# Products of queries with the rests of the keys over all 128 array rows instead of 64, in a hybrid decoder step

## The chip, the cores and the metric

The kernel runs on one core of a Trainium2 chip. The metric is the time on the device, in microseconds (us), of one execution of the whole step. The engines of the core are TensorE (PE in the profile, its weight loads PEld), VectorE (DVE), ScalarE (ACT), GpSimd (POOL) and SyncE (SP, whose queue issues most DMAs). Each engine works through its own list of instructions in order and waits for the others by semaphores.

## The reference, cut to what matters

One layer of a decoder with two branches, on a prompt of 512 tokens plus 16 learned ones, and on 8 sample sequences of 8 tokens. Two places of the prompt's attention branch concern the change. The first scores all keys for each query, to select the best 128; the second is the attention over the selected keys:

```
def indexer_scores(qi, wi, ki):
    s = jax.nn.relu(jnp.einsum('bqhd,bsd->bqhs', qi, ki) * IDX_DIM ** -0.5)
    return jnp.einsum('bqhs,bqh->bqs', s, wi * IDX_HEADS ** -0.5)
...
    s = jnp.einsum('bqhgd,bqkhd->bqhgk', qh, k_sel) * HEAD_DIM ** -0.5
    s = jnp.where(valid[:, :, None, None, :], s, -jnp.inf)
    p = jax.nn.softmax(s, axis=-1)
    o = jnp.einsum('bqhgk,bqkhd->bqhgd', p, v_sel)
```

A head has 64 elements in both (IDX_DIM and HEAD_DIM are 64). The indexer has 8 heads and one set of keys; the attention has 16 heads of queries on 4 heads of keys.

## The kernel before

**Exact products.** TensorE multiplies in float32r, which keeps fewer bits than float32. So each operand is split into a rounded part and a rest (the difference), and a product is a sum of several matmuls into one accumulator: rounded by rounded, rest by rounded, rounded by rest. For the large projections these are three matmuls of 128 rows by 288 or 296 columns (`mm3`, line 145; its like in the state space projection is line 1029).

**The two products of the change.** A head fills only 64 of the 128 rows of the array. The kernel uses this: the query tile (`qS` in the indexer, `QS` in the attention) holds the rounded query in its head's own half of the partitions and the rest of the query in the other half. One matmul with the rounded keys in both halves (`kS`, line 356; `KS`, line 963) then gives rounded by rounded and rest by rounded together, over 128 rows. A second matmul adds rounded by rest: it takes the own half of the query tile, 64 rows, against the rest of the keys (`kL`, line 357; `KL`, line 964). In the indexer `kL` has the rest in both halves of the partitions, since `kiT` was doubled. In the attention `KL` is a tile of 128 x 2 x 528, in which each half of the partitions holds one of two heads.

**The indexer** (lines 344 to 363) goes over four tiles of 128 queries, and over 144, 272, 400 and 528 keys in them, for 8 heads; 528 keys are done as pieces of 512 and 16. ACT takes the sum out of the accumulator (line 358), DVE weighs and adds it to the scores `am` (lines 360, 362), and DVE then marks the 128 highest of each row by repeated maximum and replacement (lines 420, 421). Products of the input projection (line 145) stand between on TensorE.

**The attention** (`query`, lines 926 to 1001) goes over the four tiles of queries, two pairs of key heads (`hp`), and two pairs of queries (`gp`), each with two `g` and two `e`: 64 times one row of keys, the 528 keys as pieces of 400 and 128. DVE adds the mask and takes the maximum (line 965), ACT takes the exponential (968), DVE scales (979), TensorE transposes (985, 988) and multiplies with the values (995, 996). A `Pipe` keeps units in flight. The state space projection (line 1029) fills TensorE between them; DVE adds its results up (line 1034).

**Order.** The program is built with a scheduler that lays out each engine's list from modelled times, so an added instruction can move others. Tiles come from pools: `cp` lives through the whole kernel, `pf` and `up` end when the attention begins (`u_stack.close()`).

Of the kernel before, what the change touches and what calls it, by code (L numbers as in the profile page):

```python
# [9 lines left out]
FT = mybir.dt.float32  # L10
FR = mybir.dt.float32r
# [3 lines left out]
OP = mybir.AluOpType  # L15
# [55 lines left out]
def body(ctx, tc, a, o):  # L71
    nc = tc.nc
    SB, PS, DR = bass.MemoryType.SB, bass.MemoryType.PSUM, bass.MemoryType.DRAM
    act, dve, pool, pe, sy = nc.scalar, nc.vector, nc.gpsimd, nc.tensor, nc.sync

    WB = (2, 3)
    cp = ctx.enter_context(tc.tile_pool(name="cp", bufs=1))
# [41 lines left out]

# [1 line left out]
    def split(raw, hi, lo, lo_eng=None):  # L121
# [26 lines left out]

# [1 line left out]
    def rows(src, n):  # L150
# [8 lines left out]
    pf = u_stack.enter_context(tc.tile_pool(name="pf", bufs=1, side="right"))  # L159
# [8 lines left out]
    scT = pf.tile([128, 24, 24], FT, name="scT")  # L168
    cwT = cp.tile([128, 120], FT, name="cwT")
    nwT = cp.tile([128, 16], FT, name="nwT")  # L170
    xp, xs, meta = a["x_prompt"][0], a["x_sample"].rearrange("b s d -> (b s) d"), a["meta_tokens"]
# [26 lines left out]
    for t in range(5):  # L198
# [7 lines left out]
        for q in range(2):  # L206
# [7 lines left out]
            dve.tensor_tensor(ul[:, 4 * q:4 * q + 4, 128 * t:128 * t + n], pv[:, :, :n], h_.bitcast(FT), op=OP.subtract)  # L214
    # convolution: weights and earlier rows, channels on partitions
    cwr = p0.tile([128, 128], FT, name="cwr")
# [21 lines left out]

# [1 line left out]
    d_g = drp.tile([2, 8, 128, NQ], FT, name="d_g")  # L240
# [34 lines left out]

    # page rows
    idx = cp.tile([128, 8], I32, name="idx")
    idx2 = cp.tile([128, 8, 2], I32, name="idx2")
    dts = cp.tile([128, 5, 32], FT, name="dts")
    acum = cp.tile([128, 5, 32], FT, name="acum")  # L280
    wdt = cp.tile([128, 5, 32], FT, name="wdt")
    elast = cp.tile([128, 4, 32], FT, name="elast")
    elc = cp.tile([128, 16, 8], FT, name="elc")
    dsc = cp.tile([128, 16], FT, name="dsc")
    for e in range(2):
        src = a["d_skip"]
        sy.dma_start(dsc[64 * e:64 * e + 64], bass.AP(tensor=src.tensor, offset=src.offset + e, ap=[[0, 64], [2, 16]]))
    wds = cp.tile([96, 2, 32], FT, name="wds")

    with tc.tile_pool(name="p1", bufs=1) as p1:  # L290
# [23 lines left out]

        # index queries of the prompt: the rounded part in a head's own half of the partitions, the rest in the other
        qS = p1.tile([128, 8, NP], FR, name="qS")
# [13 lines left out]

        # page rows of the sample sequences
        pt = p1.tile([128, 64], I32, name="pt")
# [10 lines left out]

# [1 line left out]
        wis = p1.tile([128, 4, 8], FT, name="wis")  # L345
        dve.tensor_scalar(wis, sm_tok[:, 0:4, 64:72], 8 ** -0.5, None, op0=OP.mult)
        for t in range(4):
            L = LT[t]
            sc = am[:, LO[t]:LO[t] + L]
            for h in range(8):  # L350
                ct, e = divmod(h, 2)
                lq, own = qS[:, h, 128 * t:128 * t + 128], slice(64 * e, 64 * e + 64)
                r = p1.tile([128, 528], FT, tag="ri", name="ri", bufs=2)
                for c0, c1 in pieces(L):
                    ps = mis()
                    pe.matmul(ps[:, :c1 - c0], lq, kS[:, c0:c1], start=True, stop=False)
                    pe.matmul(ps[:, :c1 - c0], lq[own], kL[own, c0:c1], start=False, stop=True)
                    act.activation(r[:, c0:c1], ps[:, :c1 - c0], AF.Relu, scale=0.125)
                if h == 0:
                    dve.tensor_scalar(sc, r[:, :L], wis[:, t, 0:1], None, op0=OP.mult)  # L360
                else:
                    dve.scalar_tensor_tensor(sc, r[:, :L], wis[:, t, h:h + 1], sc, op0=OP.mult, op1=OP.add)
            dve.tensor_tensor(sc[:, L - 128:L], sc[:, L - 128:L], K("neg"), op=OP.add)

# [1 line left out]
        QIz = p1.tile([128, 4, 128], FT, name="QIz")  # L366
# [47 lines left out]

# [1 line left out]
        m8 = p1.tile([128, 4, 8], FT, name="m8")  # L416
# [7 lines left out]

        # time steps and decays
        brow = p1.tile([128, 2, 32], FT, name="brow")
# [59 lines left out]

# [1 line left out]
        kvT = [KT[:, 0, :], KT[:, 1, :]]  # L488
# [15 lines left out]

# [1 line left out]
        for kp in range(8):  # L506
# [95 lines left out]

# [1 line left out]
    with tc.tile_pool(name="p3", bufs=1, reuse_waits="tile") as p3, \  # L604
# [11 lines left out]
        def start(g):  # L616
# [10 lines left out]
            pool.tensor_tensor(h8(G.xt4[64:80]), h8(G.xt4[64:80]), bc8(wdt[64:80, 4, g8], 16), op=OP.mult)  # L627
            # sample tokens: three rows of products a token, half the sequences at a time
            xb = p3s.tile([96, 2, 512], FT, tag="sT", name="xb", bufs=1)
# [177 lines left out]

# [1 line left out]
    for gt in (0, 1):  # L809
# [95 lines left out]
    with tc.tile_pool(name="p2h", bufs=1, reuse_waits="tile", side="right") as p2h, \  # L905
            tc.tile_pool(name="p2r", bufs=1, reuse_waits="tile") as p2r, \
            tc.tile_pool(name="p2q", bufs=1, reuse_waits="tile") as p2q, \
            tc.tile_pool(name="p2", bufs=1, reuse_waits="tile") as p2:
        # keys: rounded in both halves of the partitions, and the rest
        KS = p2h.tile([128, 4, 528], FR, name="KS")  # L910
        KL = p2h.tile([128, 2, 528], FR, name="KL")
        for kv in range(4):
            hp, e = divmod(kv, 2)
            h = slice(64 * e, 64 * e + 64)
            for i in range(2):
                act.copy(KS[64 * i:64 * i + 64, kv, :], KT[h, hp, 0:528])
            pool.tensor_tensor(KL[h, hp, :], KT[h, hp, 0:528], KS[h, kv, :].bitcast(FT), op=OP.subtract)

        # values of the last 16 keys of a tile: for both e in a half of the rows each, in parts for one product
        VZr = p2h.tile([32, 256], FT, name="VZr")  # L920
# [5 lines left out]
        def query(t, hp, gp):  # L926
            # queries 128t.., heads 8hp + 4e + 2gp + g
            L, nk = LT[t], t + 1
# [26 lines left out]
            for g in range(2):  # L955
                P2 = p2q.tile([128, 2, 528], FT, tag="P", name="P2", bufs=3)
                mx = p2q.tile([128, 2, 6], FT, tag="mx", name="mx", bufs=4)
                for e in range(2):
                    lq = QS[:, 2 * gp + g, e, :]
                    h = slice(64 * e, 64 * e + 64)  # L960
                    for i, (c0, c1) in enumerate(cuts):
                        v = pst("s")[:, :c1 - c0]
                        pe.matmul(v, lq, KS[:, 2 * hp + e, c0:c1], start=True, stop=False)
                        pe.matmul(v, lq[h], KL[h, hp, c0:c1], start=False, stop=True)  # L964
                        dve.tensor_tensor_reduce(P2[:, e, c0:c1], v, at[:, c0:c1], 1.0, NEG, OP.add, OP.max,
                                                 accum_out=mx[:, e, i:i + 1])
                    dve.tensor_scalar(mx[:, e, 2:3], mx[:, e, 0:1], mx[:, e, len(cuts) - 1:len(cuts)], -0.125, op0=OP.max, op1=OP.mult)
                    act.activation(P2[:, e, :L], P2[:, e, :L], AF.Exp, scale=0.125, bias=mx[:, e, 2:3],
                                   accum_out=mx[:, e, 3:4])
# [33 lines left out]
        Pipe().run(query(t, hp, gp) for t in range(4) for hp in range(2) for gp in range(2))  # L1003
# [1 line left out]
    HALVES = ((0, HQ), (HQ, NQ))  # L1005
# [38 lines left out]
    def rest(hi, lo, c0, c1):  # L1044
        # where the rest of tokens c0.. goes: that of the sample tokens beside their rounded part
        return [(lo[:, c0:min(c1, NP)], c0, min(c1, NP))] + ([(hi[:, NQ:NQ + NS], NP, NQ)] if c1 == NQ else [])
# [20 lines left out]
    y_stack.close()  # L1067
    # rows of the stream: four tiles of tokens, and the sample tokens: their sums with the rounded part, and with the rest
    p4 = ctx.enter_context(tc.tile_pool(name="p4", bufs=1, reuse_waits="tile", side="right"))
# [9 lines left out]
    def row_weights(src, r0, n, at=(p4w, ("dl", "dh"), 7)):  # L1079
        # n blocks of 128 rows of weights  # L1080
        return [[flat(x) for x in weights([(flat, src[r0 + 128 * k:r0 + 128 * k + 128, :])], at)] for k in range(n)]
# [12 lines left out]
    def row_norm(t, i):  # L1094
        # tokens of tile t and what scales them; i: column of the sums
        n = 128 if t < 4 else 64
# [42 lines left out]
    def last(t):  # L1139
        # the same by the pieces in which the last product ends  # L1140
        y, sq = h2[:, ORDER[0], :], h2[:, ORDER[1], :]
# [12 lines left out]
    def add_product(t, xh, xl, ws, cuts=((0, 512), (512, 1024))):  # L1154
        # rows of tile t += the product over blocks of channels
        tok = slice(128 * t, 128 * t + 128)
# [24 lines left out]
    p4a_stack.close()  # L1181
# [1 line left out]
    p5 = ctx.enter_context(tc.tile_pool(name="p5", bufs=1, reuse_waits="tile"))  # L1183
# [70 lines left out]
```

## Time and profile before

| | |
|---|---|
| times of the kernel before, us | 1586.87, 1586.79, 1581.91; median 1586.79 |
| the profiled execution | span 1586.9 us, the time of that run 1586.87 us |
| PE busy | 1488.5 us (94%), 9957 matmuls |
| DVE, ACT, POOL busy | 1006.5 (63%), 668.6 (42%), 721.2 us (45%) |
| the chain that ended last | PE 66%; DVE 14%; DMA 7%; ACT 4% |

Matmuls are pipelined, and the profile gives a matmul a duration from its start to its modelled end, so the durations of neighbours overlap. What a matmul costs the engine is read from the distance between its start and the start of the next one.

### The profile page before, as it was taken

What the parts mean: (1) busy time and instruction counts of PE and PEld (TensorE: products, weight loads), DVE (VectorE), ACT (ScalarE), POOL (GpSimd) and SP (SyncE); (2) the same over time, 40 slices, a digit from 0 to 9 for tenths busy, and PEclk for the clock granted to TensorE, in tenths of its full rate; (3) what the DMA queues carried; (4) which work ended last, traced back from release to release, by engine and by line L of the source; (5) the groups of instructions that cost most, each with busy time, mean ns of one, the idle gap of its engine ahead of it and who ended that gap; (6) DMA issues with size and microseconds to landing.
All of it is one profiled execution on the core that took longest, in us unless ns stands there. A gap on an engine that the chain in (4) does not pass through costs nothing.

```text
span 1586.9 us, 26540 instructions
## 1 busy us (share of the span) xinstructions
PE 1488.5 (94%) x9957; PEld 1308.9 (82%) x9957; DVE 1006.5 (63%) x1902; ACT 668.6 (42%) x1484; POOL 721.2 (45%) x641
## 2 busy tenths in 40 slices
PE   3899999899999899899999999998998999999998
PEld 2878999888878888779778877787797988998896
DVE  3579999967867776470444778765366445554544
ACT  3444354456655455343555555432144222332221
POOL 1523244556775675565534754335226334433322
PEclk8899999999999999999999999999999999999999
DMA  4413464687886886868873522135314222322311
GB/s 130 124 41 80 137 176 134 176 255 191 244 230 166 233 231 172 241 169 247 267 256 129 149 76 67 42 86 180 87 55 132 80 73 87 107 74 60 93 40 67
DMA packets 300160, 221.55 MB, mean 140 GB/s; under 512 B 46376, under 2 KB 269912, under 8 KB 300008
## 3 DMA queue, kind: packets, MB, share of 16 engines
q1 hardware_dynamic: 294784, 200.98, 44.8%
q0 software_dynamic: 5248, 18.88, 3.4%
q8 instruction: 78, 1.28, 0.3%
q14 instruction: 50, 0.41, 0.1%
HBM read 174.98 MB, written 44.07 MB: 138 GB/s over the span
## 4 chain that ended last, share of the span: by engine, by line
PE 66%; DVE 14%; DMA 7%; ACT 4%; issue 3%; POOL 1%; SPq 1%; POOLq 0%; DVEq 0%; ACTq 0%
PE w L145 19%; PE s L1166 13%; PE a L145 10%; PE w L1029 7%; DVE ca L574 3%; DMA bc<-d_ac 2%; PE s L964 2%; DVE scs L522 2%; PE s L861 2%; DVE m8s L521 1%; DVE r L1190 1%; PE s L726 1%; PE s L995 1%; PE a L985 1%; ACT wh L122 1%
## 5 line engine op out<-in xcount | busy, mean ns | idle before, releaser
L123 POOL TENSOR_TENSOR wl<-wr,wh 128x1024 fp32r<-128x1024 f32 x129 | 310.5, 2408 | 365.9 <-ACT wh L122 343.5
L145 PE MATMUL w<-uh,wh 128*128 128x288 f32 (+1 forms) x1168 | 361.9, 310 | 20.1 <-ACT rb L558 6.9
L145 PE MATMUL w<-ul,wh 128*128 128x288 f32 (+1 forms) x1168 | 359.2, 308 | 0.1
L145 PE MATMUL w<-uh,wl 128*128 128x288 f32 (+1 forms) x1168 | 355.6, 304 | 0.0
L145 PEld LDWEIGHTS w<-uh,wh 128*128 128x128 f32 x1168 | 225.3, 193 | 29.4 <-ACT rb L558 8.1
L145 PEld LDWEIGHTS w<-ul,wh 128*128 128x128 f32 x1168 | 225.7, 193 | 5.6 <-issue 4.4
L145 PEld LDWEIGHTS w<-uh,wl 128*128 128x128 f32 x1168 | 225.1, 193 | 3.8 <-issue 2.8
L122 ACT ACTIVATE wh<-wr 128x1024 fp32r<-128x1024 f32 x129 | 136.2, 1056 | 146.9 <-PE w L145 56.7
L123 POOL TENSOR_TENSOR dl<-wr,dh 128x1024 fp32r<-128x1024 f32 x40 | 99.3, 2485 | 154.6 <-ACT dh L122 149.8
L145 PE MATMUL a<-u2h,wh 128*128 128x288 f32 (+2 forms) x512 | 151.4, 296 | 0.7 <-ACT r L1189 0.7
L145 PE MATMUL a<-u2l,wh 128*128 128x288 f32 (+2 forms) x512 | 151.2, 296 | 0.0
L145 PE MATMUL a<-u2h,wl 128*128 128x288 f32 (+2 forms) x512 | 150.3, 294 | 0.0
L1168 DVE TENSOR_TENSOR h<-h,s 128x512 f32<-128x512 f32 (+1 forms) x101 | 67.1, 678 | 124.5 <-PE s L1166 123.8
L1166 PE MATMUL s<-dh,hh 128*128 128x512 f32 (+1 forms) x324 | 127.1, 393 | 5.9 <-DVE h L1168 5.9
L1166 PE MATMUL s<-dl,hh 128*128 128x512 f32 (+1 forms) x324 | 126.2, 390 | 0.0
L574 DVE SCALAR_TENSOR_TENSOR ca<-rb,cwT,ca 128x616 f32<-128x616 f32 x72 | 95.7, 1329 | 21.0 <-ACT ca L572 20.4
L122 ACT ACTIVATE dh<-wr 128x1024 fp32r<-128x1024 f32 x40 | 42.2, 1056 | 150.4 <-PE s L1166 128.7
L1190 DVE TENSOR_TENSOR r<-r 128x288 f32<-128x288 f32 (+2 forms) x64 | 70.1, 1096 | 52.6 <-ACT r L1189 52.6
L1166 PE MATMUL s<-dh,hl 128*128 128x512 f32 (+1 forms) x260 | 101.8, 392 | 0.0
L145 PEld LDWEIGHTS a<-u2h,wh 128*128 128x128 f32 x512 | 96.0, 188 | 1.5 <-ACT r L1189 0.9
L145 PEld LDWEIGHTS a<-u2l,wh 128*128 128x128 f32 x512 | 96.1, 188 | 0.6
L145 PEld LDWEIGHTS a<-u2h,wl 128*128 128x128 f32 x512 | 96.2, 188 | 0.0
(370 smaller groups left out, 3340.7 us busy)
## 6 DMA issues: line engine op xcount, KB each, us to landing
wr<-in_w_in_dram SPq DMA_DIRECT2D x64, 512.0 KB
wr<-in_w_up_dram SPq DMA_DIRECT2D x32, 512.0 KB
wr<-in_w_down_dram SPq DMA_DIRECT2D x32, 512.0 KB
st<-in_state_ssm_dram SPq DMA_DIRECT2D x16, 512.0 KB
bc<-d_ac SPq DMA_DIRECT2D x32, 256.0 KB
out_dram<-st SPq DMA_DIRECT2D x16, 512.0 KB
wr<-in_w_ssm_proj_dram SPq DMA_DIRECT2D x16, 512.0 KB
d_xd<-th SPq DMA_DIRECT2D x16, 296.0 KB
```

What stands on the lines that cost most here:

```text
L122: act.activation(hi, raw, AF.Copy)
L123: (lo_eng or pool).tensor_tensor(lo, raw, hi.bitcast(FT), op=OP.subtract)
L145: pe.matmul(ps[:, :c1 - c0], p[:, k, :], x[:, c0:c1], start=(k == 0 and i == 0), stop=(k == 7 and i == 2))
L521: dve.max(m8, scs)
L522: dve.match_replace(scs, m8, scs, MARK)
L574: dve.scalar_tensor_tensor(ca[:, 0:616], rb[:, k:k + 616], cwT[:, 24 * k + ct:24 * k + ct + 1], ca[:, 0:616], op0=OP.mult, op1=OP.add)
L861: pe.matmul(v[64 * hp:64 * hp + 64], QZ[:, hp, :], kk, start=True, stop=True)
L964: pe.matmul(v, lq[h], KL[h, hp, c0:c1], start=False, stop=True)
L1029: pe.matmul(ps[:, :HQ], p[:, k, mc], x[k][:, c0:c1], start=(k == 0 and i == 0), stop=(k == 3 and i == 2))
L1166: pe.matmul(ps, x, w[:, cc], start=(k == 0 and i == 0), stop=(k == len(ws) - 1 and i == len(terms) - 1))
L1168: dve.tensor_tensor(h2[:, t, cc], h2[:, t, cc], ps, op=OP.add)
L1190: dve.tensor_tensor(r, r, r, op=OP.mult)
```

## The change

In both places the second matmul takes the whole query tile and keys of 128 rows. In the indexer this needs no new data: the other half of `kL` holds the rest of the keys too, so the product of rest by rest comes in as a fourth part. In the attention `KL` gets a plane of its own for each of the four key heads, whose other half is filled with zeros by four memsets on POOL. Apart from this, nine small tiles (952 columns of float32 in all) move from the pool `cp` to the pool `pf`, and comments go, which shifts line numbers by one from line 351 to 915 and again from line 960.

```
-    cwT = cp.tile([128, 120], FT, name="cwT")
+    cwT = pf.tile([128, 120], FT, name="cwT")
...
-                ct, e = divmod(h, 2)
-                lq, own = qS[:, h, 128 * t:128 * t + 128], slice(64 * e, 64 * e + 64)
+                lq = qS[:, h, 128 * t:128 * t + 128]
...
                     pe.matmul(ps[:, :c1 - c0], lq, kS[:, c0:c1], start=True, stop=False)
-                    pe.matmul(ps[:, :c1 - c0], lq[own], kL[own, c0:c1], start=False, stop=True)
+                    pe.matmul(ps[:, :c1 - c0], lq, kL[:, c0:c1], start=False, stop=True)
...
         KS = p2h.tile([128, 4, 528], FR, name="KS")
-        KL = p2h.tile([128, 2, 528], FR, name="KL")
+        KL = p2h.tile([128, 4, 528], FR, name="KL")
...
-            pool.tensor_tensor(KL[h, hp, :], KT[h, hp, 0:528], KS[h, kv, :].bitcast(FT), op=OP.subtract)
+            pool.memset(KL[64 - 64 * e:128 - 64 * e, kv, :].bitcast(FT), 0.0)
+            pool.tensor_tensor(KL[h, kv, :], KT[h, hp, 0:528], KS[h, kv, :].bitcast(FT), op=OP.subtract)
...
                         pe.matmul(v, lq, KS[:, 2 * hp + e, c0:c1], start=True, stop=False)
-                        pe.matmul(v, lq[h], KL[h, hp, c0:c1], start=False, stop=True)
+                        pe.matmul(v, lq, KL[:, 2 * hp + e, c0:c1], start=False, stop=True)
```

Up to the attention no engine's list changes but for the shapes of these operands. In the attention the lists of all engines are laid out anew. On POOL, where the keys of the attention are prepared (`KL` the rests of the keys, `wl` the rest of a block of weights, `QS` the query tile), before:

```order
L123 TENSOR_TENSOR ysl<-yw,ysh 128x576
L123 TENSOR_TENSOR wl<-wr,wh 128x1024
L917 TENSOR_TENSOR KL<-KT,KS 64x528 x4
L123 TENSOR_TENSOR wl<-wr,wh 128x1024
L949 TENSOR_TENSOR QS<-R_9488,QS 64x4x128 x2
```

and now, in the same place:

```order
L123 TENSOR_TENSOR ysl<-yw,ysh 128x576
L123 TENSOR_TENSOR wl<-wr,wh 128x1024
L916 MEMSET KL 64x528 x4
L917 TENSOR_TENSOR KL<-KT,KS 64x528 x4
L123 TENSOR_TENSOR wl<-wr,wh 128x1024
L949 TENSOR_TENSOR QS<-R_9492,QS 64x4x128 x2
```

All four memsets stand in one block ahead of the four subtractions. On PE the first product of the attention, among those of the state space projection (`w` its accumulators, `ysh` and `ysl` its values, `wh` and `wl` its weights), before:

```order
L1029 MATMUL w_11410<-ysh_11234,wl_11363 128x288
L963 MATMUL s_9501<-KS_9466,QS_9489 128x144
L964 MATMUL s_9501<-KL_9467,QS_9489 128x144
L1029 MATMUL w_11430<-ysh_11216,wh_11426 128x288
L1029 MATMUL w_11430<-ysl_11217,wh_11426 128x288
```

and now:

```order
L1028 MATMUL w_11434<-ysh_11232,wl_11429 128x288
L1028 MATMUL w_11434<-ysh_11238,wh_11430 128x288
L1028 MATMUL w_11434<-ysl_11239,wh_11430 128x288
L1028 MATMUL w_11434<-ysh_11238,wl_11429 128x288
L962 MATMUL s_9505<-KS_9466,QS_9493 128x144
L963 MATMUL s_9505<-KL_9467,QS_9493 128x144
```

The accumulator `w_11434` is the `w_11430` of before (numbers are higher by four). Its block of twelve matmuls, of which the last four are shown, has moved from behind the first pair of query products to ahead of it.

## Rows read from the trace of the kernel before

**Rows 1.** The page's chain of work that ended last, by engine.

```profile
PE 66%; DVE 14%; DMA 7%; ACT 4%; issue 3%; POOL 1%; SPq 1%; POOLq 0%; DVEq 0%; ACTq 0%
```

**Rows 2.** Busy time by stretch of the execution: stretch and its length in us, then busy us (and instructions) of PE, PEld, DVE, ACT and POOL, the granted clock of TensorE, the DMA share, GB/s. The first two hold the indexer, the fifth the attention.

```profile
57.00:87.00 30.00, 26.79 (x167) 24.30 (x165) 19.33 (x40) 13.20 (x34) 14.92 (x12) 0.94 0.44 128
87.00:133.00 46.00, 46.00 (x244) 35.20 (x244) 40.23 (x116) 21.83 (x57) 11.49 (x7) 1.00 0.21 46
133.00:212.00 79.00, 78.37 (x573) 72.53 (x572) 78.62 (x175) 33.91 (x74) 22.90 (x16) 1.00 0.53 140
212.00:304.00 92.00, 87.32 (x636) 85.79 (x635) 89.36 (x102) 45.76 (x104) 45.33 (x47) 0.98 0.49 140
880.00:1036.00 156.00, 156.00 (x945) 120.20 (x945) 119.07 (x419) 81.10 (x226) 76.69 (x152) 1.00 0.27 78
970.00:980.00 10.00, 10.00 (x60) 7.02 (x59) 9.62 (x30) 5.88 (x16) 5.70 (x10) 1.00 0.23 65
304.00:312.00 8.00, 3.80 (x29) 3.56 (x27) 8.00 (x12) 1.95 (x3) 2.50 (x2) 0.96 0.51 144
312.00:320.00 8.00, 8.00 (x50) 7.07 (x51) 5.01 (x9) 4.97 (x11) 4.92 (x7) 0.62 1.00 326
```

**Rows 3.** The matmuls of lines 964 and 357 by source line: count, shortest, median and longest duration in ns, first and last start, and how often each form.

```profile
L964 PE MATMUL s<-KL,QS x80: 322/388/450, 880.5 to 1035.4; 64*128 64x400 f32 x32, 64*128 64x144 f32 x16, 64*128 64x272 f32 x16, 64*128 64x128 f32 x16
...
L357 PE MATMUL s<-kL,qS x20: 332/448/502, 61.8 to 122.3; 64*128 64x512 f32 x8, 64*128 64x144 f32 x4, 64*128 64x272 f32 x4, 64*128 64x400 f32 x4
...
L357 PE MATMUL a<-kL,qS x20: 273/330/452, 62.3 to 122.9; 64*128 64x16 f32 x8, 64*128 64x144 f32 x4, 64*128 64x272 f32 x4, 64*128 64x400 f32 x4
```

**Rows 4.** PE in order of time in the attention, a pair of 400 columns: start in us, duration, line, names, the part of the array (rows*columns), the moving operand.

```profile
960.82 0.29 PE L1029 MATMUL w<-ysh,wl 128*128 128x288 f32 x1
960.95 0.34 PE L963 MATMUL s<-KS,QS 128*128 128x400 f32 x1
961.22 0.45 PE L964 MATMUL s<-KL,QS 64*128 64x400 f32 x1
961.60 0.40 PE L1029 MATMUL w<-ysh,wh 128*128 128x288 f32 x1
961.84 0.29 PE L1029 MATMUL w<-ysl,wh 128*128 128x288 f32 x1
```

**Rows 5.** The same view in the indexer, a pair of 512 columns, and pairs of 144 and 272 in a row.

```profile
84.81 0.23 PE L356 MATMUL s<-kS,qS 128*128 128x144 f32 x1
84.96 0.33 PE L357 MATMUL s<-kL,qS 64*128 64x144 f32 x1
85.22 0.39 PE L356 MATMUL s<-kS,qS 128*128 128x272 f32 x1
85.55 0.39 PE L357 MATMUL s<-kL,qS 64*128 64x272 f32 x1
85.86 0.39 PE L356 MATMUL s<-kS,qS 128*128 128x272 f32 x1
...
110.34 0.40 PE L356 MATMUL s<-kS,qS 128*128 128x512 f32 x1
110.67 0.49 PE L357 MATMUL s<-kL,qS 64*128 64x512 f32 x1
111.09 0.40 PE L145 MATMUL w<-ul,wh 128*128 128x296 f32 x1
```

**Rows 6.** The same view near the end of the kernel, where only matmuls of 128 rows follow each other, of 512 and of 256 columns.

```profile
1574.00 0.39 PE L1166 MATMUL s<-dh,hh 128*128 128x512 f32 x1
1574.22 0.39 PE L1166 MATMUL s<-dh,hl 128*128 128x512 f32 x1
...
1576.75 0.28 PE L1166 MATMUL s<-dh,hh 128*128 128x256 f32 x1
1576.86 0.28 PE L1166 MATMUL s<-dh,hl 128*128 128x256 f32 x1
```

**Rows 7.** The same view in the attention, around a matmul of 96 rows (line 996).

```profile
927.30 0.36 PE L996 MATMUL s<-PR,VZ 96*128 96x256 f32 x1
927.50 0.30 PE L1029 MATMUL w<-ysh,wh 128*128 128x288 f32 x1
927.63 0.29 PE L1029 MATMUL w<-ysl,wh 128*128 128x288 f32 x1
```

**Rows 8.** Groups of DVE's instructions in the attention (880 to 1036 us): count, busy us, mean ns, idle time before them and what ended it.

```profile
L965 DVE CUSTOM_DVE_ANT_0 P<-s,am 128x400 f32<-128x400 f32 (+2 forms) x80 | 33.6, 432 | 13.9 <-PE s L964 11.1 <-PE a L985 1.0 <-POOL ts L977 0.7
...
L970 DVE RECIPROCAL mx<-mx 128x2 f32<-128x2 f32 x31 | 5.1, 163 | 6.8 <-ACT P L968 6.6
```

**Rows 9.** POOL in order of time where the keys are prepared, with the idle time ahead of an instruction and what ended it in brackets; and the group of the nearest memset.

```profile
868.57 1.32 POOL L917 TENSOR_TENSOR KL<-KT,KS 64x528 fp32r<-64x528 f32 x1 [0.52 <-ACT KS L916]
870.57 4.12 POOL L917 TENSOR_TENSOR KL<-KT,KS 64x528 fp32r<-64x528 f32 x3 [0.67 <-ACT KS L916]
875.60 2.40 POOL L123 TENSOR_TENSOR wl<-wr,wh 128x1024 fp32r<-128x1024 f32 x1 [0.91 <-ACT wh L122]
...
L1075 POOL MEMSET h<- 64x1024 f32 x1 | 1.0, 951 | 0.1
```

**Rows 10.** DVE in order of time, the first instruction that it waited for after the indexer (idle time ahead of it, and what ended it, in brackets).

```profile
215.69 1.70 DVE L574 SCALAR_TENSOR_TENSOR ca<-rb,cwT,ca 128x616 f32<-128x616 f32 x1 [2.20 <-ACT ca L572]
```

More of the change, by code (lines that the diff above doesn't have):

```diff
@@ L168, in body @@
     scT = pf.tile([128, 24, 24], FT, name="scT")
-    cwT = cp.tile([128, 120], FT, name="cwT")
-    nwT = cp.tile([128, 16], FT, name="nwT")
+    cwT = pf.tile([128, 120], FT, name="cwT")
+    nwT = pf.tile([128, 16], FT, name="nwT")
     xp, xs, meta = a["x_prompt"][0], a["x_sample"].rearrange("b s d -> (b s) d"), a["meta_tokens"]
@@ L278, in body @@
     idx2 = cp.tile([128, 8, 2], I32, name="idx2")
[L279 to L284, printed above, removed]
+    dts = pf.tile([128, 5, 32], FT, name="dts")
+    acum = pf.tile([128, 5, 32], FT, name="acum")
+    wdt = pf.tile([128, 5, 32], FT, name="wdt")
+    elast = pf.tile([128, 4, 32], FT, name="elast")
+    elc = pf.tile([128, 16, 8], FT, name="elc")
+    dsc = pf.tile([128, 16], FT, name="dsc")
     for e in range(2):
@@ L287, in body @@
         sy.dma_start(dsc[64 * e:64 * e + 64], bass.AP(tensor=src.tensor, offset=src.offset + e, ap=[[0, 64], [2, 16]]))
-    wds = cp.tile([96, 2, 32], FT, name="wds")
+    wds = pf.tile([96, 2, 32], FT, name="wds")
     with tc.tile_pool(name="p1", bufs=1) as p1:
@@ L959, in query @@
                     lq = QS[:, 2 * gp + g, e, :]
-                    h = slice(64 * e, 64 * e + 64)
                     for i, (c0, c1) in enumerate(cuts):
```

## The prediction

> **What bounds the kernel now.** I read the chain of waits first: two thirds of the span end in TensorE's own work [rows 1]. Then the busy times by stretch, for the two places that the change touches [rows 2]. In the attention (880 to 1036 us) PE is busy for all 156.00 us and DVE for 119.07, at full granted clock (2.4 GHz): nothing but PE's own list sets the pace. In the indexer it is mixed. From 87 to 133 us PE is full (46.00 of 46) and DVE idles for 46 - 40.23 = 5.8 us; from 133 to 212 both are full, DVE with 78.62 of 79; from 212 to 304 DVE has 89.36 of 92 and PE less. So what PE saves in the indexer runs into a DVE that is busy for the next 170 us, while what it saves in the attention goes straight to the end, as long as DVE keeps up.
>
> **What a 64-row matmul costs now.** A busy PE tells nothing here, since durations overlap; the distance between starts does. Where only 128-row matmuls follow each other, 512 columns take 0.22 to 0.23 us and 256 take 0.11 [rows 6], and 288 take 0.13 [rows 7]. The reader should now see three things around the 64-row matmul of 400 columns [rows 4]:
> - the 128-row matmul before it (L963) takes 961.22 - 960.95 = 0.27, where 400 columns are worth 0.18 (between the 0.13 of 288 and the 0.23 of 512): 0.09 too much;
> - it takes itself 961.60 - 961.22 = 0.38: 0.20 too much;
> - the next (L1029) takes 961.84 - 961.60 = 0.24 instead of 0.13: 0.11 too much.
>
> Together 0.40 us for a pair. The third is the telling one: L1029 has no operand or accumulator in common with the query products, and pays for standing behind one. Behind the 96-row matmul of line 996, which the profile gives as 96*128, the same L1029 takes 0.13 [rows 7]. So it is the step to 64 rows and back that costs: PE ends what it has before it loads the next weights. The Trainium skill has a rule that speaks against a gain (TensorE: Matmul & The Clock Gate, Why this matters for your kernels): a single matmul of few rows takes the same time as one of 128. By that rule the sum below would be 0; by rows 4 it is 0.40 a pair. No row here shows 64-row matmuls behind each other; where the two kinds alternate, the trace doesn't bear the rule out.
>
> The other sizes in the same way. For 272 columns, between two 64-row ones, L356 takes 0.33 and L357 0.31 [rows 5], both worth 0.13 at 128 rows: 0.20 + 0.18, about 0.39. For 512, 0.33 and 0.42 against 0.23 each [rows 5], and 0.11 behind it: 0.40. For 144, 0.15 and 0.26 [rows 5]; no row shows so short a product among 128-row ones, so I take the 0.11 of 256 columns as its floor: 0.04 + 0.15 + 0.11 = 0.30; for 128 the same. For the 16-wide pieces of the indexer I take half of 0.40, an estimate.
>
> **The change, part by part.**
> - *Attention, second product over 128 rows.* 32 pairs of 400, 16 of 272, 16 of 144, 16 of 128 [rows 3]: 32 x 0.40 + 16 x 0.39 + 32 x 0.30 = 28.6 us of PE's 156. That leaves 127.4, and DVE's 119.07 below it [rows 2]. DVE's waits for PE shrink with it (11.1 us for L964 alone), but its waits for ACT's exponential do not: 6.8 us before the reciprocal [rows 8]. 119.1 + 6.8 = 125.9, just under PE's 127.4, and in 970 to 980 us DVE already has 9.62 of 10 [rows 2]. Two engines so nearly even, tied in order through three accumulators, won't both run without a gap. I charge 1.2 us for that stretch (9.62 less the 8.4 that PE would want with four pairs of 400 shortened) and half of the 6.8, 3.4 us: 28.6 - 4.6 = 24. Bounds: 28.6 if DVE hides all, 14 if half is lost.
> - *Indexer, second product over 128 rows.* 8 pairs each of 512, 400, 272, 144 and 16 columns [rows 3]: 8 x (0.40 + 0.40 + 0.39 + 0.30 + 0.20) = 13.5 us of PE. What is late next is DVE. The first pairs, from 61.8 us on, fall where PE also waits for others (26.79 busy of 30 [rows 2]); from 87 us on, DVE can come forward by no more than its idle 5.8 us, and, at 215.69, by the 2.20 us in which it waited for ACT [rows 10]. So 0 to 13.5, and I take 6, near DVE's idle time.
> - *Four memsets on POOL.* The nearest row is 0.95 us for 64 x 1024 [rows 9], so 0.5 each for 64 x 528, 2 us in a block ahead of the four subtractions. POOL finished its weights at about 868.0 and waited 0.52 and 0.67 for ACT's KS; the subtractions took 5.4 [rows 9]. With the memsets first they run from 870.1 to 875.5 instead of to 874.7, and the weights behind them started at 875.60, after 0.91 of waiting for ACT [rows 9]. So nothing moves: the cover is that wait, and without it the cost is at most 2 us, once, for the weights and query tile queued behind it. The memsets wait for PE's last reads of the memory they write, as ACT's KS does; a longer wait would go the same way.
> - *Order.* The block of twelve matmuls ahead of the first query product is work that PE does anyway; at about 875 to 880 us it only gives POOL's query tile more time. Bounds of the new lists as a whole: 2 us either way, and I take 0. The tiles that changed pools are read and written as before: 0.
>
> **Sum.** The profiled execution took 1586.87 us with a span of 1586.9, so nothing lies around the span, and it stands at the median of 1586.79 (the lowest of the three runs is 1581.91). 1586.9 - 24 - 6 = 1557 us.
>
> **Rivals.**
> - *PE's saving arrives in full.* 28.6 + 13.5 = 42: 1545 us. For it: DVE's work that PE needs is a small part in the indexer, most is the marking of the best keys, which nobody needs before the attention. Against it: DVE does its list in order, and PE's needs stand between.
> - *DVE becomes the bound in both places.* Half of the attention's 28.6 and nothing of the indexer: 1573 us. For it: DVE at 0.76 of the attention's time and 0.99 of 133 to 212 us. Against it: a third of DVE's idle time in the attention is a wait for the very product that gets shorter [rows 8].
> - *The row count is not what costs.* Then the second product over 128 rows would stop the engine as the one over 64 does, because of its accumulator or its repeated query tile, and the time stays within 2 us of 1587. For it: only query products show the 0.38, and always in such pairs. Against it: the L1029 behind a pair shares neither with it and pays 0.11 [rows 4], but nothing behind 96 rows [rows 7]. The Trainium skill's rule above would give the same 1587.
> - *TensorE's clock falls in the attention: slower.* After 304 to 312 us, in which PE was busy for only 3.80 of 8, it was granted 0.62 in the mean of the next 8 us, so most of them at 1.2 GHz instead of 2.4 [rows 2]. If PE now waits for DVE in the attention and half of its 127.4 us of work comes at 0.62, it takes 63.7 + 63.7 / 0.62 = 166, 10 us more than now; with 6 from the indexer, 1591. It decides from a mean below 127.4 / (156 + 6) = 0.79. Against it: PE would still be busy for nine tenths of the stretch, and 212 to 304 us, with PE that busy, stands at 0.98 [rows 2].
>
> **How the numbers follow.** The forecast as summed has a chance of 0.62, with a range of its own of 1549 to 1565; the full saving 0.12; DVE as the bound 0.18; the row count without effect 0.05; the slower clock 0.03. The range of 1545 to 1573 takes in the first three. About 0.3% (5 us) is what a measurement of this kernel tells from no change: faster than that 0.92, within it 0.05, slower 0.03.
>
> **What would show it.** The start-to-start distances: L962 and L963 of 400 columns at 0.18 each and the following projection matmul at 0.13; the attention at about 132 us from its first query product to its last, instead of 155; the PE-paced start of the state space part at 304 us some 6 us earlier, with DVE without idle time between 87 and 212. It is wrong if a matmul behind the second product still takes 0.24 (then it was not the rows), or if those distances are right but PE shows waits for DVE's L964 or L978 that add up to more than 14 us (then DVE is the bound).

## The result, and the profile after

The changed kernel takes 1548.93 us (median of 4 runs, 1545.86 to 1551.57), the kernel before 1585.62 on the same chip (4 runs): a ratio of 0.9775, 95% interval 0.9755 to 0.9794. That is 36.7 us less; the prediction had 30 less, 1557, and a range of 1545 to 1573. The time lies inside that range, and at the edge of the narrower one that the sum had of its own (1549 to 1565). The profiled execution of the changed kernel took 1551.57 us, with a span of 1549.8.

The first view is the chain of work that ended last. Against [rows 1] the share that ends in PE has fallen from 66 to 58%, and DVE's has grown from 14 to 19%:

```profile
PE 58%; DVE 19%; DMA 8%; ACT 5%; issue 4%; SPq 2%; POOL 2%; POOLq 0%; DVEq 0%; ACTq 0%
```

Busy time by stretch, columns as in [rows 2]; the first four hold the indexer and what follows it, the last the attention:

```profile
57.00:82.00 25.00, 21.70 (x148) 21.29 (x149) 18.75 (x36) 10.82 (x28) 13.01 (x10) 0.93 0.50 148
82.00:122.00 40.00, 38.05 (x256) 35.07 (x255) 37.07 (x111) 23.31 (x60) 9.94 (x6) 1.00 0.21 43
122.00:202.00 80.00, 79.07 (x576) 73.17 (x575) 79.62 (x181) 33.50 (x73) 25.30 (x18) 1.00 0.53 145
202.00:296.00 94.00, 88.48 (x641) 86.76 (x640) 91.33 (x102) 45.94 (x105) 45.05 (x49) 0.98 0.48 136
867.00:997.00 130.00, 129.13 (x948) 114.72 (x947) 115.92 (x416) 78.36 (x226) 76.84 (x152) 1.00 0.33 94
```

The attention's two engines are now nearly even, 129 us of PE and 116 of DVE in 130, and PE still waits for nothing to speak of (0.87 us). The second products by source line, as in [rows 3], show the stretch: from 867.8 to 995.8 it is 128.0 us, where it was 154.9.

```profile
L963 PE MATMUL s<-KL,QS x80: 272/290/432, 867.8 to 995.8; 128*128 128x400 f32 x32, 128*128 128x144 f32 x16, 128*128 128x272 f32 x16, 128*128 128x128 f32 x16
...
L356 PE MATMUL s<-kL,qS x20: 229/343/396, 63.3 to 110.9; 128*128 128x512 f32 x8, 128*128 128x144 f32 x4, 128*128 128x272 f32 x4, 128*128 128x400 f32 x4
```

PE in order of time around a pair of 400 columns, which answers to [rows 4], and around a pair of 128 columns:

```profile
942.65 0.29 PE L1028 MATMUL w<-ysl,wh 128*128 128x288 f32 x1
942.78 0.34 PE L962 MATMUL s<-KS,QS 128*128 128x400 f32 x1
942.96 0.34 PE L963 MATMUL s<-KL,QS 128*128 128x400 f32 x1
943.14 0.29 PE L1028 MATMUL w<-ysh,wl 128*128 128x288 f32 x1
943.28 0.29 PE L1028 MATMUL w<-ysh,wh 128*128 128x288 f32 x1
...
962.58 0.22 PE L962 MATMUL s<-KS,QS 128*128 128x128 f32 x1
962.64 0.27 PE L963 MATMUL s<-KL,QS 128*128 128x128 f32 x1
962.75 0.35 PE L1028 MATMUL w<-ysh,wh 128*128 128x288 f32 x1
962.94 0.27 PE L987 MATMUL a<-cst,ts 128*96 128x128 f32 x1
```

From start to start the pair of 400 takes 0.18 and 0.18, and the projection matmul behind it 0.14 (942.78, 942.96, 943.14, 943.28): the 0.27, 0.38 and 0.24 of [rows 4] are gone, by 0.39 us in all. The pair of 128 takes 0.06 and 0.11, and what stands behind it 0.19: the weight loads (PEld) of this stretch start 0.11 to 0.14 us apart, more than the 0.06 that 128 columns take, so part of the cost stays. In the indexer, as in [rows 5]:

```profile
82.99 0.23 PE L355 MATMUL s<-kS,qS 128*128 128x144 f32 x1
83.06 0.28 PE L356 MATMUL s<-kL,qS 128*128 128x144 f32 x1
83.17 0.33 PE L355 MATMUL s<-kS,qS 128*128 128x272 f32 x1
83.34 0.28 PE L356 MATMUL s<-kL,qS 128*128 128x272 f32 x1
83.46 0.29 PE L355 MATMUL s<-kS,qS 128*128 128x272 f32 x1
...
101.94 0.39 PE L355 MATMUL s<-kS,qS 128*128 128x512 f32 x1
102.17 0.40 PE L356 MATMUL s<-kL,qS 128*128 128x512 f32 x1
102.41 0.30 PE L145 MATMUL w<-ul,wh 128*128 128x296 f32 x1
```

512 columns take 0.23 and 0.24, 144 take 0.07 and 0.11. DVE's groups in the attention (867 to 997 us), as in [rows 8], show that its wait for the query products has all but gone, from 13.9 to 1.9 us, and that for ACT's exponential has stayed:

```profile
L964 DVE CUSTOM_DVE_ANT_0 P<-s,am 128x400 f32<-128x400 f32 (+2 forms) x79 | 31.9, 429 | 1.9 <-PE s L963 1.5 <-POOL ts L976 0.4
...
L969 DVE RECIPROCAL mx<-mx 128x2 f32<-128x2 f32 x31 | 5.1, 163 | 7.3 <-ACT P L967 7.1
```

POOL where the keys are prepared, and the first wait of DVE after the indexer, which answer to [rows 9] and [rows 10]:

```profile
854.12 2.25 POOL L916 MEMSET KL<- 64x528 f32 x4
856.34 5.58 POOL L917 TENSOR_TENSOR KL<-KT,KS 64x528 fp32r<-64x528 f32 x4
861.99 2.41 POOL L123 TENSOR_TENSOR wl<-wr,wh 128x1024 fp32r<-128x1024 f32 x1
```

```profile
205.92 1.69 DVE L573 SCALAR_TENSOR_TENSOR ca<-rb,cwT,ca 128x616 f32<-128x616 f32 x1 [2.23 <-ACT ca L571]
```

The four memsets take 2.25 us, and the subtractions follow without a wait. DVE's wait for ACT at the start of the convolution, 2.20 us before, is 2.23 now: it came forward with everything else and gave nothing back.

### The profile page after: what moved, and what is told of

Its sections match the earlier page's. It is cut to its first block, busy times and chain, and to the rows that moved or that the text cites. A ratio compares the mean times of both kernels' runs of the same rounds, so it can differ in the third digit from the quotient of the medians.

```text
span 1549.8 us, 26550 instructions
## 1 busy us (share of the span) xinstructions
PE 1455.0 (94%) x9957; PEld 1302.2 (84%) x9957; DVE 1005.0 (65%) x1902; ACT 665.6 (43%) x1484; POOL 722.3 (47%) x645
## 4 chain that ended last, share of the span: by engine, by line
PE 58%; DVE 19%; DMA 8%; ACT 5%; issue 4%; SPq 2%; POOL 2%; POOLq 0%; DVEq 0%; ACTq 0%
PE s L1165 16%; PE w L145 12%; PE a L145 11%; PE w L1028 6%; DVE ca L573 3%; DVE scs L521 2%; PE s L860 2%; DVE m8s L520 2%; DVE am L420 1%; DMA bc<-d_ac 1%; DVE am L361 1%; DVE m L419 1%; DVE r L1189 1%; ACT wh L122 1%; PE s L725 1%
## 5 line engine op out<-in xcount | busy, mean ns | idle before, releaser
L1167 DVE TENSOR_TENSOR h<-h,s 128x512 f32<-128x512 f32 (+1 forms) x101 | 67.2, 678 | 128.0 <-PE s L1165 126.9
L122 ACT ACTIVATE dh<-wr 128x1024 fp32r<-128x1024 f32 x40 | 42.4, 1059 | 154.9 <-PE s L1165 132.1
```

What stands on the lines that cost most here:

```text
L122: act.activation(hi, raw, AF.Copy)
L1167: dve.tensor_tensor(h2[:, t, cc], h2[:, t, cc], ps, op=OP.add)
```

## The experiments

The table has what was read from each run: the time and its ratio to the runs of before of the same chip, and from the profiled execution the last indexer product into an accumulator `s` (line 357; the one into `a` comes 0.2 to 0.7 us later), the last marking of the sample scores (522), the time from there to the first copy of the attention's keys (916), from that copy to the last product with the values (996), and from there to the last product of the feed-forward (1166, hidden by rounded weights). All are starts, in us, and lines are those of before. Before itself took 1585.30 us on the chip of e1 to e4 (13 runs), 1586.72 on that of e5, e7, d1 and d2 (17) and 1584.88 on that of e8 and e9 (9).

| run | time (runs) | ratio, 95% interval | last indexer product | last marking | to key copy | attention | behind it |
|---|---|---|---|---|---|---|---|
| before | 1585.62 (4) | | 122.3 | 308.0 | 559.9 | 175.9 | 535.3 |
| after | 1548.93 (4) | 0.9775, 0.9755 to 0.9794 | 110.9 | 299.5 | 554.4 | 149.6 | 538.8 |
| e1 indexer alone | 1577.83 (10) | 0.9959, 0.9933 to 0.9986 | 111.0 | 298.4 | 558.8 | 175.9 | 532.2 |
| e2 attention alone | 1559.58 (4) | 0.9833, 0.9785 to 0.9881 | 120.7 | 306.8 | 555.6 | 149.7 | 538.6 |
| e3 rows alone | 1552.95 (4) | 0.9788, 0.9732 to 0.9844 | 110.3 | 297.4 | 559.2 | 152.3 | 536.5 |
| e4 both on 64 rows | 1569.93 (2) | 0.9899, 0.9835 to 0.9962 | 117.3 | 302.8 | 559.1 | 165.8 | 535.7 |
| e5 tiles alone | 1585.39 (12) | 1.0000, 0.9981 to 1.0018 | 122.8 | 308.9 | 556.1 | 176.2 | 537.7 |
| e7 rows and tiles | 1553.24 (6) | 0.9801, 0.9768 to 0.9834 | 110.1 | 298.0 | 559.5 | 152.1 | 540.1 |
| d1 few marks, 64 rows | 1588.73 (1) | | 120.2 | 279.8 | 587.9 | 175.9 | 536.0 |
| d2 few marks, 128 rows | 1581.29 (1) | | 109.3 | 268.1 | 590.4 | 176.0 | 537.6 |
| e8 96 rows | 1550.09 (1) | | 110.5 | 297.5 | 553.1 | 150.9 | 539.4 |
| e9 after again | 1552.14 (5) | 0.9789, 0.9768 to 0.9811 | 109.5 | 297.5 | 555.1 | 151.0 | 538.0 |

**Each place alone.** The kernel before with the indexer's second product on 128 rows:

```
-                    pe.matmul(ps[:, :c1 - c0], lq[own], kL[own, c0:c1], start=False, stop=True)
+                    pe.matmul(ps[:, :c1 - c0], lq, kL[:, c0:c1], start=False, stop=True)
```

> Kernel before with the 128-row second product in the indexer alone. My theory (stepping from 128 to 64 rows and back costs about 0.4 us a pair, and DVE's list takes part of what TensorE saves here): 8 to 11 us faster than before, about 1576; the attention unchanged, 155 us from its first query product to its last. Rival (TensorE's 13.5 us arrive in full): 13 to 14 us faster. Rival (DVE takes it all): no change.

and the changed kernel with that line, and the two that serve it, put back as before:

```
-                lq = qS[:, h, 128 * t:128 * t + 128]
+                ct, e = divmod(h, 2)
+                lq, own = qS[:, h, 128 * t:128 * t + 128], slice(64 * e, 64 * e + 64)
...
-                    pe.matmul(ps[:, :c1 - c0], lq, kL[:, c0:c1], start=False, stop=True)
+                    pe.matmul(ps[:, :c1 - c0], lq[own], kL[own, c0:c1], start=False, stop=True)
```

> The changed kernel with the indexer's second product back at 64 rows. Theory: 27 us faster than before (24 to 30), about 1558; 128 us from the first to the last query product of the attention, and the stretch before it as in the kernel before. If the two places were not independent, the gains of this run and of the indexer alone would not add up to the 36 us of the whole change.

The indexer alone gave 0.41% (1585.30 to 1577.83 us), 7.5 us, just under the 8 to 11 that I had expected; the attention alone 1.67% (to 1559.58), 25.7 us, within the 24 to 30. Together 2.08%, some 33 us: within the interval of the whole change, 2.06 to 2.45%, at its lower end, and neither needs the other. In the table each shortens its own stretch by as much as both do: the last indexer product comes at 111.0 with and without the attention's half, the attention takes 149.7 and 149.6 us with and without the indexer's.

**The rows without what goes with them.** The kernel before with the two matmuls widened, and nothing else: `KL` keeps its two planes, so that the other half of the rows holds the rests of the other head's keys, under the rests of the query. No zeros, no memsets, no tiles moved, and the order of before. It adds the product of the rests of the query with the rests of another head's keys, which the reference doesn't have.

```
-                    pe.matmul(ps[:, :c1 - c0], lq[own], kL[own, c0:c1], start=False, stop=True)
+                    pe.matmul(ps[:, :c1 - c0], lq, kL[:, c0:c1], start=False, stop=True)
...
-                        pe.matmul(v, lq[h], KL[h, hp, c0:c1], start=False, stop=True)
+                        pe.matmul(v, lq, KL[:, hp, c0:c1], start=False, stop=True)
```

> The kernel before with nothing but the two matmuls widened to 128 rows: in the attention the other half of the rests then belongs to the other key head, so a product of rest by rest of two different heads is added, which is tiny; no memsets, no larger tile, no tiles moved between pools. Theory (the rows alone make the gain): the time of the changed kernel, 1549, within 3 us. Rival (the new order of the attention, the memsets or the pools have a part in the gain): 4 us or more away from it, on either side.

1552.95 us, 0.9788: two shapes of operands carry the gain. The 4.0 us to the 1548.93 of the changed kernel are just over the 3 that I had allowed, but that one was measured beside other runs of before; the two ratios lie within each other's intervals, and so does that of the changed kernel measured again (e9, below). By source line its second products span 131.6 us, against 128.0 with the new order and 154.9 before:

```profile
L964 PE MATMUL s<-KL,QS x80: 272/289/351, 869.2 to 1000.8; 128*128 128x400 f32 x32, 128*128 128x144 f32 x16, 128*128 128x272 f32 x16, 128*128 128x128 f32 x16
```

**Both products on 64 rows.** If it is the step between 64 and 128 rows that costs, a pair that stays on 64 rows should pay it once in and once out, and where a pair stands right behind another, not between them. The version leaves out the product of the rest of the query with the rounded keys, in both places:

```
-                    pe.matmul(ps[:, :c1 - c0], lq, kS[:, c0:c1], start=True, stop=False)
+                    pe.matmul(ps[:, :c1 - c0], lq[own], kS[own, c0:c1], start=True, stop=False)
...
-                        pe.matmul(v, lq, KS[:, 2 * hp + e, c0:c1], start=True, stop=False)
+                        pe.matmul(v, lq[h], KS[h, 2 * hp + e, c0:c1], start=True, stop=False)
```

> The kernel before with both products of a pair over 64 rows; the product of the rest of the query with the rounded keys is left out. Theory (the cost is that of the step in and out, once a pair): the time of before within 6 us, and the first product of a pair followed by the second at 0.18 us for 400 columns. Rival (each 64-row matmul pays for itself): the first product takes about 0.38 too, 120 more such matmuls, 25 to 40 us slower than before.

It took 1569.93 us, 15.4 less than before on the same chip. I had expected the time of before within 6 us, and had not thought of the pairs that follow each other. PE in order of time, a lone pair and then two pairs in a row:

```profile
972.09 0.39 PE L996 MATMUL s<-PR,VZ 96*128 96x256 f32 x1
972.40 0.45 PE L963 MATMUL s<-KS,QS 64*128 64x400 f32 x1
972.69 0.34 PE L964 MATMUL s<-KL,QS 64*128 64x400 f32 x1
972.96 0.40 PE L1029 MATMUL w<-ysl,wh 128*128 128x288 f32 x1
973.20 0.30 PE L1029 MATMUL w<-ysh,wl 128*128 128x288 f32 x1
...
1000.18 0.34 PE L964 MATMUL s<-KL,QS 64*128 64x400 f32 x1
1000.36 0.21 PE L963 MATMUL s<-KS,QS 64*128 64x128 f32 x1
1000.42 0.27 PE L964 MATMUL s<-KL,QS 64*128 64x128 f32 x1
```

Going in, the first 64-row product takes 972.69 - 972.40 = 0.29 instead of 0.18, 0.11 more; going out, the last takes 0.27, 0.09 more, and the L1029 behind it 0.24 instead of 0.13, 0.11 more. The 96-row matmul ahead of the pair pays the 0.09 as well: 972.40 - 972.09 = 0.31, where 0.22 is its distance to a 128-row product in the run on 96 rows below. So each change of row count costs 0.20 us: 0.09 on the matmul that ends and 0.11 on the one that begins. The weight loads of before show what is lost there, around the pair of [rows 4]:

```profile
960.82 0.19 PEld L963 LDWEIGHTS s<-KS,QS 128*128 128x128 f32 x1
961.22 0.18 PEld L964 LDWEIGHTS s<-KL,QS 64*128 64x128 f32 x1 [0.21 <-issue]
961.60 0.19 PEld L1029 LDWEIGHTS w<-ysh,wh 128*128 128x128 f32 x1 [0.20 <-issue]
```

The weights of L963 are loaded from 960.82 on, 0.13 ahead of their matmul (960.95). Those of the 64-row product, and those of L1029 behind it, start only with their matmuls (961.22 and 961.60), after PEld has idled for 0.2. On 128 rows in the changed kernel the load of the second product starts at 942.78, 0.18 ahead of its matmul. A lone 64-row matmul pays two such changes, which is the 0.40 of [rows 4]; a 64-row product behind another of the same head takes 0.18 for 400 columns and 0.06 for 128 (1000.18, 1000.36, 1000.42), as on 128 rows. In before 24 of the attention's 80 pairs stand right ahead of another, and 12 of the 40 of the indexer; 24 x 0.40 = 9.6 and 12 x 0.40 = 4.8 us should go, and the table has 175.9 - 165.8 = 10.1 for the attention and 122.3 - 117.3 = 5.0 for the indexer.

That agreement is in part luck. The changes of row count are not all that went: where two pairs in a row belong, by the order of the kernel's loops, to the two heads `e`, which lie on opposite halves of the rows, they run side by side; the pieces of one head (400 and 128 columns, 512 and 16) run behind each other. A view of such a place (x2 stands for two matmuls in a row of the same names):

```profile
965.03 0.29 PE L1029 MATMUL w<-ysh,wh 128*128 128x288 f32 x1
965.25 0.45 PE L963 MATMUL s<-KS,QS 64*128 64x400 f32 x2
965.54 0.34 PE L964 MATMUL s<-KL,QS 64*128 64x400 f32 x2
965.82 0.40 PE L1029 MATMUL w<-ysl,wh 128*128 128x288 f32 x1
```

The two first products start within 0.01 us of each other, and so do the two second ones; two pairs take 965.82 - 965.25 = 0.57, and the lone pair above took 972.96 - 972.40 = 0.56. There are 16 such places in the attention of e4 and 6 in its indexer. At what a pair of its columns takes on 128 rows in e3 (0.21 to 0.37), the second pairs of the 16 are worth some 4 of the 10.1 us, an estimate. Some 6 are left for the changes of row count, less than 9.6, since not every pair costs 0.40: the 80 of before cost 25.8 us more than those of e3 (counted below), 0.32 in the mean. The lists of e4 were laid out anew as well, and no run takes the two effects apart.

**How many rows count as whole.** The changed kernel with the even heads' second products on 96 rows; the rows left out hold zeros.

```
-                        pe.matmul(v, lq, KL[:, 2 * hp + e, c0:c1], start=False, stop=True)
+                        p = slice(0, 128 if e else 96)
+                        pe.matmul(v, lq[p], KL[p, 2 * hp + e, c0:c1], start=False, stop=True)
```

> The changed kernel, with the second attention product of the even heads (e = 0) over 96 of the 128 rows, 40 of its 80 pairs; the rows left out hold zeros. Theory A (what costs is the step between a product that the profile gives as 64 rows and one that it gives as 128; 96 rows count as the whole array): the time of the changed kernel, 1546 to 1554 us, L963 of 400 columns at 0.18 us to the next start and the projection matmul behind it at 0.13, over 96 rows as over 128. Rival B (every count below 128 makes TensorE stop): the 40 pairs pay 0.35 to 0.40 us each again, 14 to 16 us, so 1562 to 1567, and the matmul behind a 96-row product takes 0.24.

```profile
943.73 0.38 PE L996 MATMUL s<-PR,VZ 96*128 96x256 f32 x1
943.95 0.34 PE L962 MATMUL s<-KS,QS 128*128 128x400 f32 x1
944.13 0.35 PE L964 MATMUL s<-KL,QS 96*128 96x400 f32 x1
944.32 0.30 PE L1029 MATMUL w<-ysh,wh 128*128 128x288 f32 x1
944.46 0.29 PE L1029 MATMUL w<-ysl,wh 128*128 128x288 f32 x1
```

1550.09 us, one run; 0.18, 0.19 and 0.14 from start to start, as on 128 rows. The 96-row product is free of the step and rival B falls.

**Is DVE late in the indexer?** Two versions in which 12 of the 16 marking rounds of the prompt's scores are left out, the first as before, the second with the indexer's second product on 128 rows as above:

```
-            for _ in range(TOP_P // 8):
+            for _ in range(TOP_P // 32):
```

> The kernel before, with 4 of the 16 marking rounds that DVE makes for each of the prompt's score tiles in the indexer; the other 12 are left out, so the selection is of fewer keys. It makes DVE light in the indexer and is the base for the next run; by itself it only shows how much of the indexer's span is DVE's: the last indexer product (122.3 us in before) is expected between 112 and 121 us.

> The same cut of marking rounds, with the indexer's second products on 128 rows. Theory A (DVE takes part of what the rows save in the indexer, 8.5 to 10.6 us of the 13.5 to 14 that TensorE spends less): with DVE light the last indexer product comes 12.5 to 14 us earlier than in the run with the same cut on 64 rows. Rival B (the rest is lost in the waits for the queries' casts ahead of 85 us, which do not hang on the marking rounds): it comes 9 to 11 us earlier, as with all rounds.

The last indexer product in both, the first key copy in the first, and that version's busy time from 131 to 204 us:

```profile
L357 PE MATMUL s<-kL,qS x20: 330/448/502, 61.7 to 120.2; 64*128 64x512 f32 x8, 64*128 64x144 f32 x4, 64*128 64x272 f32 x4, 64*128 64x400 f32 x4
...
L916 ACT CAST KS<-KT x8: 630/632/635, 867.7 to 872.2; 64x528 fp32r<-64x528 f32 x8
```

```profile
L357 PE MATMUL s<-kL,qS x20: 230/342/397, 62.1 to 109.3; 128*128 128x512 f32 x8, 128*128 128x144 f32 x4, 128*128 128x272 f32 x4, 128*128 128x400 f32 x4
```

```profile
131.00:204.00 73.00, 69.93 (x498) 64.10 (x498) 50.34 (x70) 34.12 (x76) 19.95 (x10) 0.98 0.49 131
```

The last product comes 120.2 - 109.3 = 10.9 us earlier, as it does with all the rounds (11.3 in e1): theory A falls, and the number is rival B's. The first key copy tells the same: 867.7 - 858.5 = 9.2 us earlier with DVE light, 867.9 - 857.2 = 10.7 with all the rounds. The first run alone says more than I had asked of it. DVE is busy for 50.34 of 73 us where it had been full, its last marking comes 28 us earlier (279.8), and yet the first key copy stands at 867.7, against 867.9 in before, and the time at 1588.73. An engine that was 99% busy was not what set the pace: PE, at 78.37 of 79 us [rows 2], was. (The lists of all engines were laid out anew for this version, so it isn't before with less DVE work and nothing else.)

**The tiles that changed pools.** From the last marking to the key copy the changed kernel takes 554.4 us and e2 555.6, but before 559.9, e1 558.8, e3 559.2: some 4 us that nothing in the prediction accounts for. The instructions there are the same in all of them, and what differs is where nine tiles lie. Before with nothing but these tiles moved, and e3 with them moved as well:

```
-    cwT = cp.tile([128, 120], FT, name="cwT")
-    nwT = cp.tile([128, 16], FT, name="nwT")
+    cwT = pf.tile([128, 120], FT, name="cwT")
+    nwT = pf.tile([128, 16], FT, name="nwT")
...
-    dts = cp.tile([128, 5, 32], FT, name="dts")
+    dts = pf.tile([128, 5, 32], FT, name="dts")
...
```

> The kernel before with nine small tiles of the state-space part allocated in the pool that the change moves them to; both second products stay on 64 rows and every engine's list of instructions is the one of before. Theory A (where these tiles lie is worth the 4 us by which the stretch from the last marking round of the indexer to the first copy of the attention's keys is shorter in the changed kernel, 554.4 us there, and in the run with the attention's half alone, 555.6, than in the three runs without the moves, 558.8 to 559.9): that stretch is 554 to 556 us and the time 1580 to 1582. Rival B (those 4 us belong to single executions, or to the larger key buffer): the stretch is 558 to 561 us and the time is that of before, 1584 to 1587.

> The version with only the two products widened (the rests of both heads of a pair under the rest of each query, no zeros written, the order of before), with the nine tiles moved as well. It leaves nothing out; beside the wanted sums it adds the product of the two rests. Theory A (the tiles' place is worth 4 us): 1548 to 1550, as the changed kernel. Rival B (it is worth nothing): 1551 to 1554, as the run of the rows alone. A third view (the zeros and the two planes more cost something that the moves hide): 1545 to 1547, faster than the changed kernel.

The first came out at the stretch of theory A (556.1) and the time of rival B: a ratio of 1.0000, interval 0.9981 to 1.0018, over 12 runs. The second had rival B's stretch (559.5) and its time. The moves are worth nothing within 3 us. Last, the changed kernel itself once more, no edit:

> The changed kernel as it is, beside the same number of runs of before, to compare with the two versions that widen the products without zeros (1552.95 and 1553.24 us, ratios 0.9788 and 0.9801). Theory A (its zeros and the order that comes with them gain nothing in the time; the 2 us by which its attention is shorter are given back behind): ratio 0.979 to 0.981, 1552 to 1555 where before takes 1586. Rival B (the new order of the attention is worth 2 to 4 us): ratio 0.976 to 0.978, 1548 to 1551. For the stretch between the last marking round and the first key copy, 554 to 560 us are expected, whatever it was in the first execution, if its length is a matter of the single execution.

1552.14 us, ratio 0.9789: theory A by the ratio, at its lower edge. Its stretch is 555.1, and 553.1 in e8. So with the tiles moved five executions of six lie between 553.1 and 556.1, without them all between 558.8 and 559.9 (the two with few marks left aside); a tendency of the profiled executions, which the times of e5 and e7 don't bear out. It stays open.

No version is shown to beat the changed kernel: e3, e7 and e9 stand at 0.9788, 0.9801 and 0.9789, well inside each other's intervals. The two widened operands alone do as much as the change.

## Why the prediction was right, and where its sum was off

*A 64-row matmul among 128-row ones costs 0.40 us.* Right for 272 to 512 columns (0.39 to 0.40 where a projection matmul follows), and now shown from four sides: the distances after, the shapes alone in e3, the split at a lone pair of e4, the 96 rows of e8. The rival that the row count is not what costs has fallen: the same products, with the same accumulators and repeated query tiles, run through at 128 rows. The Trainium skill's rule (TensorE: Matmul & The Clock Gate, Why this matters for your kernels), that a single matmul of few rows takes the time of one of 128, agrees with e4 where 64-row products of one head follow each other (0.18 for 400 columns), and not with [rows 4], where the two kinds alternate (0.38).

*Attention, 28.6 us of PE less 4.6 for DVE, 24.* The result is near, 23.6 to 26.3 by the table (175.9 less 152.3 to 149.6), but by luck: both terms were too large, and the two errors cancel. The distances of all 80 pairs in order of time add up to 46.7 us in before and 25.0 in e3, which has the same order: 21.7 less. The matmul behind a pair gives another 4.1: 0.11 behind 17 pairs of 400 columns and 9 of 272, but only 0.06 behind 15 short ones, and 0.03 to 0.06 where one of 12 transposes follows. That is 25.8, not 28.6. Of it 154.9 - 131.6 = 23.3 arrive in e3 from the first `KL` product to the last, mostly because PE waits there where it did not in before, the longest time for DVE:

```profile
PE w L1029 <- DVE ms L1034: 1.3, 1, 1.3
```

With two shorter waits it is 1.9 us, and a matmul behind a wait takes about 0.1 longer. So some 2 of the 4.6 that I charged came with the order of before, and in the changed kernel PE idled for 0.87 in all. DVE's idle time before the query products' sums fell by 12 us, and its wait for ACT, the 6.8 us of which I charged half, stayed at 7.3 without holding PE up. The rival with DVE as the bound would have shown waits of PE for DVE of more than 14 us; it falls.

*Indexer, 6 us.* This is the step that failed, "What is late next is DVE". By the medians of the distances in order of time PE saves 8 x (0.61 + 0.39 + 0.42 + 0.25) = 13.4 us there, for 512 with its 16, 400, 272 and 144 columns, as good as the 13.5 of the prediction; PE's idle time between 57 us and the end of the stretch grew from 8.5 (30 - 26.79, 79 - 78.37, 92 - 87.32 in [rows 2]) to 11.7 (the first four rows of the same view after), 3.2 more. What PE waits for from 82 to 122 us, where before has no wait from 87 to 133, is not DVE but ACT's ReLU, which takes the sums out of the accumulators (line 357, its result `ri`):

```profile
PE a L355 <- ACT ri L357: 1.2, 1, 1.2
PE s L451 <- ACT ri L357: 0.6, 1, 0.6
```

All six runs with 128 rows there and all marking rounds have these 1.8 to 1.9 us, and none with 64 rows and all rounds (before, e2, e4, e5) has them. The waits for the parts of the queries (`qS` and `qis`), rival B's reason, are 2.4 to 3.2 us in before, e2 and e5 and 3.5 to 4.7 in the six. 13.4 - 3.2 = 10.2, and the last marking comes 8.5 to 10.6 us earlier in the six runs with 128 rows there and all marking rounds. I had read a DVE at 78.62 of 79 us as the next bound. But PE was as full beside it, and the idle time of DVE that I had counted, 5.8 and 2.2 us, leaves out 10.7 of 30 in the first stretch. It still idles for 2.9 of 40 us from 82 to 122 us, where I expected none. d1 shows that DVE's load there doesn't decide.

*Memsets 0, tiles 0, order within 2 us.* Right as far as the times show it: e3 has none of the three and stands where e9 does. The new order makes the attention itself 1 to 2.5 us shorter (149.6 to 151.0 against 152.1 and 152.3).

*The clock.* Granted 1.00 in the mean of the attention (867 to 997 us), so the slower rival did not come; PE idled there for only 0.87 us.

*Sum.* About 10 from the indexer and 24 to 26 from the attention are 34 to 36. The stretch behind the attention took 536.5 to 540.1 us in the runs with the wide attention and 532.2 to 537.7 in the others, in the mean 3 more; the two sets overlap, and why was not tried. That leaves 31 to 33, and e3, e7 and e9 have 32.4, 33.5 and 32.7 (each against before on its chip). The 36.7 of the first four runs has an interval of 32.7 to 38.8, whose lower end agrees. Against the predicted 30 it is 4 more from the indexer and 1 from the attention, less the 3 behind it, so it is in part luck that the sum came so near. The rival of the saving in full had 1545, nearer to the first 1548.93 than the forecast is, but it isn't what happened either: by the distances the full saving is 25.8 + 13.4 = 39.2 us.

## What to carry to other kernels

Look at the part of the array of each matmul in order of time: where 64-row products stand alone between 128-row ones, count the changes of row count, not the rows. Fill the other half, with data that belongs there or with zeros, or put the 64-row products behind each other: that took away the changes between them, and where two of them lay on opposite halves of the rows they ran side by side, which a count of changes does not hold. And an engine that is 99% busy need not be the bound where another beside it is as full: ask in which of the two the waits end.

## What the runs showed of the hardware that I had not expected

- The price of a change has two parts on two matmuls: 0.09 us on the one that ends and 0.11 on the one that begins, also when the latter shares nothing with it; the same from 96 to 64 rows.
- A product of 128 or 144 columns on 128 rows can take as little as 0.06 to 0.07 us to the next start, where I had taken 0.11 as the floor; those behind it then take longer, 0.11 the second of the pair and 0.18 to 0.24 a projection matmul.
- Two 64-row products on opposite halves of the rows run side by side: two pairs of 400 columns take 0.57 us in e4, one pair 0.56.
